# Finer background steps, weight splits shared with GpSimd, second buffers and earlier spatial operands in a hybrid gMLP and DeltaNet layer

## The chip, the cores and the metric

The program runs on one core of one Trainium2 chip. The metric is the device time of one execution, in microseconds (us); the kernel before took 2707.07 us, the median of three runs (2705.86, 2707.07, 2707.12). PE is TensorE, DVE is VectorE, ACT is ScalarE, POOL is GpSimd, and SP is the engine from whose queue the transfers are issued.

## The reference

One layer of a decoder works on 2048 new tokens of one sequence and on one new token of each of 8 other requests (the samples), with 1024 features. All products are in float32.

```python
h = rmsnorm(x, pre_g)
u_a, v_a, z_a, qkv, z_b, a_b, b_b, gate_a, gate_b = split(h @ w_in)
# branch A: inside chunks of 128 positions, 8 groups of 128 channels
vn = rmsnorm(v_a); y_a = u_a * (tril(w_s) @ vn + b_s) * silu(z_a)
# branch B: 8 heads of width 128
q, k, v = silu(causal_conv4(qkv)); q, k = l2norm(q) / sqrt(128), l2norm(k)
for t: S = a_t * S; S += k_t beta_t (v_t - S.T k_t).T; o_t = S.T q_t
y_b = rmsnorm(o) * silu(z_b)
out = x + rmsnorm((sigmoid(gate_a) * (y_a @ w_pa) + sigmoid(gate_b) * (y_b @ w_pb)) @ w_out)
```

The states, the last convolution rows and the samples' outputs are returned as well.

## The kernel before, in words

**The stream.** The bulk of PE's work is a stream of jobs. A job multiplies one 128-column block of a weight by the activations of half the tokens. Float32 is reached with three products in a rounded type: the weight is split into `hi` and `lo`, the activations into `Ah` and `Al`, and for each of 8 pieces of the 1024 features (k) `products` (L151) runs hi with Ah, hi with Al, and lo with Ah into one PSUM tile `acc` (L161). Half 0 has 1024 tokens, in two token blocks of 512 columns; half 1 has 1024 tokens and the 8 samples, in three blocks of 344. `split` (L141) makes `hi` on ACT (L147) and `lo` on DVE in two pieces of 128x512 (L149), for the next job, while the second token block of the present one runs. There are 185 splits.

**Background rounds.** Everything else is written as generators that yield between steps. `products` counts the columns that it has streamed, and each time the count passes `STRIDE` (2800) it calls `step`, which advances each of four queues once: `chq` (the chain), `smq` (statistics and samples), `cvq` (convolutions) and `bgq` (the rest, in order). Matrix products and transposes keep the program order on PE; a scheduler places the other engines' instructions, and from its own model it also sets how many `acc` products stand ahead of a background product.

**What runs in the background.** Per half: `v_mix` (L376), the spatial products of branch A. For each of 8 groups it fetches a triangular weight `wst` and a bias `bb` over the SP queue, masks `wst` on POOL (L407), scales a 128x1024 tile of v by its norm on POOL (L410), then runs four 128x128 products into `mx`, finishes them on DVE as `mo` (L418) and stores them. Then 8 heads, one after another (`head`, L424): transposes of k and q (`trn`), decays, key products `pk` (three products per chunk of 128 tokens, whose operands `kh` and `kl` are parted one chunk ahead on ACT L480 and POOL L481; `M` and `AT` come from `pk` on DVE, L494 and L495), scaling of q by the decays on POOL (L497), the inverse of a unit triangle (31 rounds of L511, L512, L513 on DVE, spread over 28 yields), and the merges (`g`, `p` and the POOL copies of `X`, L538 and L556). The merges start when `chq` is empty. The chain (L573) of a head then runs beside the next head: for each of 8 chunks three steps, `p` (product with the state S, then `r` on DVE, L585), `pz` (then `w` on ACT, L591) and `pu` (then the state S on DVE, L596), one step per round; after four chunks the output is normed, turned (`otr`) and finished as `yT` on DVE (L615), six rounds later.

```python
            yield
            pz = pg.tile([P, P], F32, tag="ch", name="pz", bufs=2)
            mm(pz, Y[:, c, :], r, start=True, stop=True)
            mm(O[:, n, :], qT[:, t], Sh, start=True, stop=False)
```

The convolutions of k, q and v run on DVE (L650, L653). In branch A the mixed rows are multiplied by silu(z) on POOL (L685). `samples` (L727) handles the 8 single tokens near the end. The opening (`v_phase`, L870, with L933 and L946) computes v of the first half while the first norms are still being made (`pr`, L245), and an end phase (from L1066, with L1100 and L1101) forms the outputs.

Of the kernel before, what the change touches and what calls it, by code (L numbers as in the profile page):

```python
# [15 lines left out]
P = 128  # L16
KB = 8
NH = 8
# [6 lines left out]
STRIDE = 2800  # L25
# [3 lines left out]
def hybrid_step(tc, d):  # L29
# [111 lines left out]
    def split(j):  # L141
        if j.hi is None:
            load(j)
            j.hi = wp.tile([P, KB, P], F32R, tag="hi", name="hi")
            j.lo = wp.tile([P, KB, P], F32R, tag="lo", name="lo")
            m = j.m
            nc.scalar.activation(j.hi[:, :, :m], j.raw[:, :, :m], AF.Copy)  # L147
            for p in (slice(0, 4), slice(4, 8)):
                nc.vector.tensor_tensor(j.lo[:, p, :m], j.raw[:, p, :m], j.hi[:, p, :m].bitcast(F32), ALU.subtract)  # L149
# [130 lines left out]
    # ======================= main phase =======================  # L280
# [4 lines left out]
    def btile(tag, dt=F32, shape=(P, 8, P)):  # L285
        return sp.tile(list(shape), dt, tag=tag, name=tag, bufs=2 if tag == "AT" else 1)
# [3 lines left out]
    # the 16 columns of a and b  # L290
# [85 lines left out]
    def v_mix(f, vts, ssv, sv):  # L376
        xv = sp.tile([P, 8], F32, tag="xv", name="xv")
        rv = sp.tile([P, 8], F32, tag="rv", name="rv")
        nc.vector.tensor_reduce(xv, ssv.rearrange("p (n g) -> p n g", n=8), AX.X, ALU.add)
        nc.vector.tensor_scalar(xv, xv, 1.0 / 1024, EPS, ALU.mult, ALU.add)  # L380
        rsqrt(rv, xv, 8)
        yield
        if f:
            sq = sp.tile([P, 64], F32, tag="sq", name="sq")
            nc.scalar.activation(sq, sv.rearrange("p g b -> p (g b)"), AF.Square)
            pc = pg.tile([P, 512], F32, tag="tr", name="pc")
            st = sp.tile([P, 16], F32, tag="st", name="st")[:, 0:NS]
            nc.vector.tensor_reduce(st, sq.rearrange("p (g b) -> p b g", b=NS), AX.X, ALU.add)
            yield
            mm(pc[:, 0:NS], ones, st, start=True, stop=True)  # L390
            xs = sp.tile([P, NS], F32, tag="xs", name="xs")
            rs = sp.tile([P, NS], F32, tag="rs", name="rs")
            nc.vector.tensor_scalar(xs, pc[:, 0:NS], 1.0 / 1024, EPS, ALU.mult, ALU.add)
            rsqrt(rs, xs, NS)
            nc.vector.tensor_tensor(sv, sv, rs.unsqueeze(1).to_broadcast([P, 8, NS]), ALU.mult)
            nc.vector.tensor_tensor(sv, sv, gmlpg.unsqueeze(2).to_broadcast([P, 8, NS]), ALU.mult)
            dma(d["o_vr"], sv)
            ms = sp.tile([P, 8, NS], F32, tag="ms", name="ms")
            nc.vector.tensor_tensor(ms, sv, ws00.unsqueeze(2).to_broadcast([P, 8, NS]), ALU.mult)
            nc.vector.tensor_tensor(ms, ms, bs0.unsqueeze(2).to_broadcast([P, 8, NS]), ALU.add)  # L400
            for g in range(8):
                dma(m_sp[f][g][:, HALF:HALF + NS], ms[:, g, :])
            yield
        for g in range(8):
            wst = sp.tile([P, P], F32, tag="r", name="wst", bufs=2)
            dma(wst, d["ws"][g])
            nc.gpsimd.affine_select(wst, wst, [[1, P]], ALU.is_ge, 0.0, base=0, channel_multiplier=-1)  # L407
            bb = sp.tile([P, P], F32, tag="w", name="bb", bufs=2)
            dma(bb, d["bs"][g:g + 1, :].partition_broadcast(P))
            nc.gpsimd.tensor_tensor(vts[g], vts[g], rv.unsqueeze(2).to_broadcast([P, 8, P]), ALU.mult)  # L410
            for _ in range(7 if g == 0 else 1):
                yield
            for gi in range(2):
                mx = pg.tile([P, 512], F32, tag="o" if gi == 0 else "kq", name="mx")
                for n in range(4):
                    mm(mx[:, n * P:(n + 1) * P], vts[g][:, gi * 4 + n, :], wst, start=True, stop=True)
                mo = sp.tile([P, 512], F32, tag="yT", name="mo", bufs=2)
                nc.vector.scalar_tensor_tensor(mo.rearrange("p (n t) -> p n t", t=P), mx.rearrange("p (n t) -> p n t", t=P), gmlpg[:, g:g + 1],  # L418
                                               bb.unsqueeze(1).to_broadcast([P, 4, P]), ALU.mult, ALU.add)
                dma(m_sp[f][g][:, gi * 512:(gi + 1) * 512], mo)  # L420
                yield

# [1 line left out]
    def head(f, h, T):  # L424
# [52 lines left out]
        def parted(c):  # L477
            kh = sp.tile([P, 2, P], F32R, tag="kh", name="kh", bufs=2)
            kl = sp.tile([P, 2, P], F32R, tag="kl", name="kl", bufs=2)
# [5 lines left out]
        yield  # L485
        for c in range(8):
            kh, kl = parts.pop()
            if c < 7:
                parted(c + 1)
# [10 lines left out]
        # inverse of the unit triangle: 32-blocks by substitution, then merged  # L500
# [8 lines left out]
        for l in range(31):  # L509
# [4 lines left out]
            if (l + 1) * 28 // 31 > l * 28 // 31:  # L514
                yield
# [3 lines left out]
        while chq:  # L519
            yield  # L520
        Y = btile("Y")
# [51 lines left out]
    def chain(f, h, kT, qT, KD, NV, AT, Y, T, bb, fe, eg, so):  # L573
        hcf = hc[f]
        col = lambda n, c: hcf[n][:, c * 8 + h:c * 8 + h + 1]
        Sh = S[:, h, :]
        for gi in range(2):
            O = pg.tile([P, 4, P], F32, tag="o", name="O")
            for n in range(4):
# [6 lines left out]
                yield  # L586
# [5 lines left out]
                yield  # L592
# [4 lines left out]
                yield  # L597
# [11 lines left out]
            for _ in range(6):  # L609
                yield  # L610
# [12 lines left out]
    def conv_job(f, kind, h, acts, T, after=None):  # L623
# [11 lines left out]
        def evac(b, ps, off, w):  # L635
# [5 lines left out]
            if f:  # L641
                nc.gpsimd.tensor_copy(qs[:, blk, :], raw[:, HALF + 3:HALF + 3 + NS])
            cvq.append(conv(raw))
# [18 lines left out]
    def zb_job(f, h, acts, T):  # L662
        def pre():
            T["zb"] = sp.tile([P, 1032], F32, tag="zb", name="zb", bufs=1)

        def evac(b, ps, off, w):
            zb = T["zb"]
            nc.scalar.activation(zb[:, off:off + w], ps[:, :w], AF.Silu)
            if b == 2 and f:
                nc.gpsimd.tensor_copy(zbs[:, h, :], zb[:, HALF:HALF + NS])  # L670

# [55 lines left out]
    def samples():  # L727
        while "E" not in ended:
# [45 lines left out]
        # pairs (k, q) per head and sample  # L774
# [40 lines left out]
        yield  # L815
        nc.vector.tensor_tensor(sq[:, 0:64], o, o, ALU.mult)
# [52 lines left out]
    # v of the first half comes with tokens on the partitions, straight from the products  # L869
    def v_phase(A, vt_tile, st):  # L870
        spans = [(0, 1), (1, 2), (2, 4), (4, 6), (6, 8)]
        tags = [("Y", 1), ("NV", 1), ("KD", 2), ("KD", 2), ("craw", 2), ("craw", 2), ("AT", 2), ("vT", 1)]
# [15 lines left out]
        def stage(cv, i):  # L888
            if i == 0:
                t = flat(wp.tile([P, KB, P], F32, tag="raw", name="raw", bufs=1))  # L890
            elif cv == 0 and i == 1:
                t = sp.tile([P, 1032], F32, tag="zb", name="wraw")
# [95 lines left out]
    def half(f):  # L988
# [7 lines left out]
        def vt_tile(g):  # L996
# [4 lines left out]
            return sp.tile([P, 1032], F32, tag="zb", name="vt7", bufs=1)[:, 0:HALF].rearrange("p (n c) -> p n c", c=P)  # L1001
# [63 lines left out]
    # ======================= end phase =======================  # L1065
# [179 lines left out]
```

## Time and profile before

| what | value |
|---|---|
| runs | 2705.86, 2707.07, 2707.12 us |
| profiled execution, span | 2705.5 us |
| PE busy | 2615.8 us (97%), 15755 matmuls |
| DVE busy | 1553.0 us (57%) |
| ACT busy | 1044.4 us (39%) |
| POOL busy | 420.7 us (16%) |
| mean granted TensorE clock | 0.987 of full speed |

The profiled execution took 2705.5 us from its first instruction to its last; the median of the runs is 1.6 us above that span. Busy times are sums over the instructions of an engine; the clock is what the throttle granted TensorE, as a share of full speed.

### The profile page before, as it was taken

How to read it: one execution, taken by the hardware profiler on the slowest of the kernel's cores; microseconds unless marked ns; L12 is line 12 of the kernel's file. 1: busy time of each engine (PE TensorE's matmuls, PEld its weight loads, DVE VectorE, ACT ScalarE, POOL GpSimd, SP SyncE). 2: the span in 40 equal slices, each digit the busy share in tenths (PEclk: the TensorE clock that was granted, in tenths of full speed). 3: DMA queues.
4: the chain of work that ended last, by engine and by line, in shares of the span. 5: the costliest groups of instructions: out<-in, count | busy, mean ns of one | idle time of the engine just before them, and what ended most of it. 6: DMA issues, size and time to landing. Idle time of an engine off the chain costs nothing.

```text
span 2705.5 us, 42484 instructions
## 1 busy us (share of the span) xinstructions
PE 2615.8 (97%) x15755; PEld 2334.3 (86%) x15755; DVE 1553.0 (57%) x5001; ACT 1044.4 (39%) x2728; POOL 420.7 (16%) x535
## 2 busy tenths in 40 slices
PE   7989999999999999989999999999998999999998
PEld 6778788887788888989999999999998988999886
DVE  6266866765765725356668657567565444442454
ACT  5323453453453423423534534534431332332121
POOL 2021111121121102022112211211202102102000
PEclk9989999999999999999999999999999999999999
DMA  6232212211211223123122122112145676645442
GB/s 205 79 121 63 67 43 71 86 44 59 79 44 67 86 77 115 48 70 108 56 65 68 48 76 72 42 68 75 46 133 202 221 245 233 243 168 183 136 141 95
DMA packets 139792, 280.38 MB, mean 104 GB/s; under 512 B 19944, under 2 KB 75688, under 8 KB 139584
## 3 DMA queue, kind: packets, MB, share of 16 engines
q1 hardware_dynamic: 139584, 277.66, 31.0%
q8 instruction: 124, 2.03, 0.3%
q14 instruction: 84, 0.69, 0.1%
HBM read 205.06 MB, written 72.55 MB: 103 GB/s over the span
## 4 chain that ended last, share of the span: by engine, by line
PE 78%; DVE 11%; DMA 5%; ACT 3%; issue 1%; POOL 1%; SPq 0%; DVEq 0%; ACTq 0%; POOLq 0%
PE acc L161 64%; PE p L32 2%; PE acc L933 2%; PE O L32 2%; DVE vT L653 2%; PE trn L33 2%; PE pu L32 1%; PE g L32 1%; DVE lo L149 1%; PE pz L32 1%; PE pk L32 1%; DMA m<-mo 1%; DVE bc L511 1%; DVE nwt L96 1%; DMA xt<-in_x_tok 1%
## 5 line engine op out<-in xcount | busy, mean ns | idle before, releaser
L161 PE MATMUL acc<-Ah,hi 128*128 128x344 f32 (+1 forms) x3360 | 1202.2, 358 | 1.4 <-ACT Ah L203 1.4
L161 PE MATMUL acc<-Ah,lo 128*128 128x344 f32 (+1 forms) x3360 | 1201.0, 357 | 0.3 <-DVE lo L149 0.3
L161 PE MATMUL acc<-Al,hi 128*128 128x344 f32 (+1 forms) x3360 | 1199.4, 357 | 0.5 <-DVE Al L204 0.2
L161 PEld LDWEIGHTS acc<-Al,hi 128*128 128x128 f32 x3360 | 636.1, 189 | 57.7 <-DVE Al L204 1.4
L161 PEld LDWEIGHTS acc<-Ah,lo 128*128 128x128 f32 x3360 | 636.6, 189 | 57.1 <-DVE lo L149 0.6
L161 PEld LDWEIGHTS acc<-Ah,hi 128*128 128x128 f32 x3360 | 636.2, 189 | 57.1 <-ACT Ah L203 1.9
L149 DVE TENSOR_TENSOR lo<-raw,hi 128x512 fp32r<-128x512 f32 x370 | 266.3, 739 | 313.4 <-ACT hi L147 278.8
L147 ACT ACTIVATE hi<-raw 128x1024 fp32r<-128x1024 f32 x185 | 195.3, 1056 | 320.6 <-PE acc L161 282.8
L513 DVE TENSOR_TENSOR Yc<-Yc,tmp 128x248 f32<-128x248 f32 (+30 forms) x496 | 148.6, 300 | 10.2
L511 DVE STREAM_SHUFFLE bc<-Uc 128x248 f32<-128x248 f32 (+30 forms) x496 | 151.1, 309 | 0.0
L512 DVE TENSOR_TENSOR tmp<-bc,Yc 128x248 f32<-128x248 f32 (+30 forms) x496 | 145.7, 294 | 0.5
L481 POOL TENSOR_TENSOR kl<-kq,kh 128x256 fp32r<-128x256 f32 x128 | 97.9, 773 | 238.1 <-ACT kh L480 237.9
L653 DVE SCALAR_TENSOR_TENSOR kq<-craw,convw,kq 128x1024 f32<-128x1024 f32 x96 | 122.6, 1277 | 1.1
L591 ACT ACTIVATE w<-pz,s_bb 128x128 f32<-128x128 f32 x128 | 46.9, 367 | 184.4 <-PE pz L32 184.1
L585 DVE SCALAR_TENSOR_TENSOR r<-p,neg,NV 128x128 f32<-128x128 f32 x128 | 44.2, 346 | 126.7 <-PE p L32 126.2
L161 PE MATMUL acc<-Bh,hi 128*128 128x344 f32 (+1 forms) x320 | 111.9, 350 | 0.0
L161 PE MATMUL acc<-Bh,lo 128*128 128x344 f32 (+1 forms) x320 | 111.9, 350 | 0.0
L161 PE MATMUL acc<-Bl,hi 128*128 128x344 f32 (+1 forms) x320 | 111.6, 349 | 0.0
L1101 POOL TENSOR_TENSOR g<-g,u 128x344 f32<-128x344 f32 (+1 forms) x40 | 45.1, 1128 | 349.1 <-DVE g L1100 344.9
L637 ACT ACTIVATE craw<-acc 128x344 f32<-128x344 f32 (+1 forms) x120 | 61.1, 509 | 94.1 <-PE acc L161 93.8
L446 ACT ACTIVATE junk<-trn 128x128 f32<-128x128 f32 x256 | 67.4, 283 | 42.3 <-PE trn L33 42.3
L1100 DVE TENSOR_TENSOR g<-g,acc 128x344 f32<-128x344 f32 (+1 forms) x40 | 23.2, 581 | 101.6 <-PE acc L161 83.5
(321 smaller groups left out, 3485.3 us busy)
## 6 DMA issues: line engine op xcount, KB each, us to landing
raw<-in_w_blk SPq DMA_DIRECT2D x136, 512.0 KB, 3.7
g<-big SPq DMA_DIRECT2D x16, 516.0 KB, 3.2
g<-g SPq DMA_DIRECT2D x16, 516.0 KB, 4.8
xt<-in_x_tok SPq DMA_DIRECT2D x16, 512.0 KB, 4.8
m<-mo SPq DMA_DIRECT2D x32, 256.0 KB, 3.1
G<-gc SPq DMA_DIRECT2D x16, 512.0 KB, 9.0
g<-big SPq DMA_DIRECT2D x16, 512.0 KB, 2.8
yb<-yT SPq DMA_DIRECT2D x32, 256.0 KB, 2.3
```

The source lines that it names most:

```text
L32: mm = lambda *a, **k: tc.keep_in_program_order(nc.tensor.matmul(*a, **k))
L33: transpose = lambda *a, **k: tc.keep_in_program_order(nc.tensor.transpose(*a, **k))
L147: nc.scalar.activation(j.hi[:, :, :m], j.raw[:, :, :m], AF.Copy)
L149: nc.vector.tensor_tensor(j.lo[:, p, :m], j.raw[:, p, :m], j.hi[:, p, :m].bitcast(F32), ALU.subtract)
L161: nc.tensor.matmul(out, wt[:, k, :j.m], at[:, k, off:off + w], start=(i == 0), stop=(i == 23))
L446: nc.scalar.activation(junk, tr[:, tk(n)], AF.Square, accum_out=acc[:, c:c + 1])
L481: nc.gpsimd.tensor_tensor(kl, kq[:, :, tk(c)], kh.bitcast(F32), ALU.subtract)
L511: nc.vector.stream_shuffle(bc[:, :, l + 1:], Uc[:, :, l + 1:], [l] * 32)
L512: nc.vector.tensor_tensor(tmp[:, :, l + 1:], bc[:, :, l + 1:], Yc[:, :, l:l + 1].to_broadcast([P, 8, 31 - l]), ALU.mult)
L513: nc.vector.tensor_tensor(Yc[:, :, l + 1:], Yc[:, :, l + 1:], tmp[:, :, l + 1:], ALU.subtract)
L637: nc.scalar.activation(raw[:, 3 + off:3 + off + w], ps[:, :w], AF.Copy)
L653: nc.vector.scalar_tensor_tensor(acc, raw[:, i:i + HALF], convw[:, blk, i:i + 1], acc, ALU.mult, ALU.add)
```

## The change

- `STRIDE` falls from 2800 to 2000 columns, so background rounds come more often. The chain yields `LAG` = 2 times where it yielded once, and waits 8 rounds where it waited 6.
- In `split` the second piece of `lo` (k 4 to 7) is made by GpSimd and no longer by DVE.
- `Y`, `NV` and `zb` have two buffers, `kh` and `kl` three, and the key operands are parted two chunks ahead.
- The inverse yields after each of its 31 rounds. The merges of a head start when one chain or none is left in `chq`, and no longer when none is.
- `v_mix` fetches the operands of group g+1 before the products of group g, and yields evenly, twice per group.
- `samples` waits on flags for what it reads, since its order against the rest is looser. The last lines free some SBUF for the buffers.

```diff
-STRIDE = 2800
+STRIDE = 2000
+LAG = 2
...
-            for p in (slice(0, 4), slice(4, 8)):
-                nc.vector.tensor_tensor(j.lo[:, p, :m], j.raw[:, p, :m], j.hi[:, p, :m].bitcast(F32), ALU.subtract)
+            for eng, p in ((nc.vector, slice(0, 4)), (nc.gpsimd, slice(4, 8))):
+                eng.tensor_tensor(j.lo[:, p, :m], j.raw[:, p, :m], j.hi[:, p, :m].bitcast(F32), ALU.subtract)
...
-        return sp.tile(list(shape), dt, tag=tag, name=tag, bufs=2 if tag == "AT" else 1)
+        return sp.tile(list(shape), dt, tag=tag, name=tag, bufs=2 if tag in ("AT", "Y", "NV") else 1)
...
-        for g in range(8):
+        def fetch(g):
             wst = sp.tile([P, P], F32, tag="r", name="wst", bufs=2)
...
-            for _ in range(7 if g == 0 else 1):
+            return wst, bb
+
+        yield
+        got = fetch(0)
+        for _ in range(8):
+            yield
+        for g in range(8):
+            wst, bb = got
+            if g < 7:
+                got = fetch(g + 1)
+            for gi in range(2):
                 yield
-            for gi in range(2):
...
-            kh = sp.tile([P, 2, P], F32R, tag="kh", name="kh", bufs=2)
-            kl = sp.tile([P, 2, P], F32R, tag="kl", name="kl", bufs=2)
+            kh = sp.tile([P, 2, P], F32R, tag="kh", name="kh", bufs=3)
+            kl = sp.tile([P, 2, P], F32R, tag="kl", name="kl", bufs=3)
...
         parted(0)
         yield
+        parted(1)
+        yield
         for c in range(8):
-            kh, kl = parts.pop()
-            if c < 7:
-                parted(c + 1)
+            kh, kl = parts.pop(0)
+            if c < 6:
+                parted(c + 2)
...
-            if (l + 1) * 28 // 31 > l * 28 // 31:
+            if True:
                 yield
...
-        while chq:
-            yield
+        while len(chq) > 1:
+            yield
+        yield
...
+        def lag():
+            for _ in range(LAG):
+                yield
+
...
-                yield
+                yield from lag()
                 pz = pg.tile([P, P], F32, tag="ch", name="pz", bufs=2)
...
-            for _ in range(6):
+            for _ in range(8):
                 yield
             tr = pg.tile([P, 512], F32, tag="tr", name="otr")
...
-            T["zb"] = sp.tile([P, 1032], F32, tag="zb", name="zb", bufs=1)
+            T["zb"] = sp.tile([P, 1032], F32, tag="zb", name="zb", bufs=2)
...
-        while "E" not in ended:
+        while "E" not in ended or any(("qs", b) not in ended for b in range(24)):
             yield
...
-    nc = bacc.Bacc("TRN2", target_bir_lowering=False, num_devices=1)
+    nc = bacc.Bacc("TRN2", target_bir_lowering=False, num_devices=1, dynamic_dma_scratch_size=1024)
```

The instruction streams show three things that the diff does not. In the changed kernel line numbers are higher: L149, L161, L410 and L933 of before are L150, L162, L411 and L955. First, PE in a chain of half 0: `p` is the product with the state, `pz` the next step, whose operand `r` DVE makes in between; `acc` are the stream's products. Before:

```order
L32 MATMUL p_2835<-S,kq 128x128
L161 MATMUL acc<-Al,hi 128x512
L161 MATMUL acc<-Ah,lo 128x512
L161 MATMUL acc<-Ah,hi 128x512
L161 MATMUL acc<-Al,hi 128x512
L161 MATMUL acc<-Ah,lo 128x512
L32 MATMUL pz<-r,Y 128x128
```

And with the change:

```order
L33 MATMUL p_3222<-S,kq 128x128
L162 MATMUL acc<-Ah,hi 128x512
L162 MATMUL acc<-Al,hi 128x512
L162 MATMUL acc<-Ah,lo 128x512
L162 MATMUL acc<-Ah,hi 128x512
L162 MATMUL acc<-Al,hi 128x512
L162 MATMUL acc<-Ah,lo 128x512
L162 MATMUL acc<-Ah,hi 128x512
L162 MATMUL acc<-Al,hi 128x512
L33 MATMUL pz<-r,Y 128x128
```

Eight products of the stream stand between two chain steps where five stood (five or six in most places before, eight now). Second, POOL around the scaling of v in half 0, before:

```order
L204 TENSOR_TENSOR Al<-big,Ah 128x256 x4
L410 TENSOR_TENSOR E<-E,rv 128x1024
L410 TENSOR_TENSOR G<-G,rv 128x1024
L410 TENSOR_TENSOR M<-M,rv 128x1024
L410 TENSOR_TENSOR AT<-AT,rv 128x1024
L410 TENSOR_TENSOR Y<-Y,rv 128x1024
L410 TENSOR_TENSOR NV<-NV,rv 128x1024
L410 TENSOR_TENSOR vt_721<-vt_721,rv 128x1024
L410 TENSOR_TENSOR vt_722<-vt_722,rv 128x1024
L640 COPY hist<-craw 128x3
```

And with the change:

```order
L205 TENSOR_TENSOR Al<-big,Ah 128x256 x4
L535 MEMSET Y 128x1024
L150 TENSOR_TENSOR lo<-raw,hi 128x512 x2
L411 TENSOR_TENSOR E<-E,rv 128x1024
L411 TENSOR_TENSOR G<-G,rv 128x1024
L411 TENSOR_TENSOR M<-M,rv 128x1024
L411 TENSOR_TENSOR AT<-AT,rv 128x1024
L411 TENSOR_TENSOR Y<-Y,rv 128x1024
L411 TENSOR_TENSOR NV<-NV,rv 128x1024
L411 TENSOR_TENSOR vt_721<-vt_721,rv 128x1024
L411 TENSOR_TENSOR vt_722<-vt_722,rv 128x1024
L150 TENSOR_TENSOR lo<-raw,hi 128x512
```

The eight scalings still stand in one row on POOL, and pieces of `lo` have come in ahead of them and behind them. Third, PE in the opening: `pr` spreads the norms of the last tokens over the partitions, and `acc` with `wvhi`, `wvlo`, `wvh` and `wvl` are the first half's v. The last `pr` of the opening, before:

```order
L933 MATMUL acc_525<-wvhi_172,Ah_168 128x512
L933 MATMUL acc_525<-wvhi_172,Al_169 128x512
L933 MATMUL acc_525<-wvlo_174,Ah_168 128x512
L32 MATMUL pr_546<-cst_72,rx_81 128x128 x2
L933 MATMUL acc_525<-wvhi_172,Ah_168 128x512
```

And with the change:

```order
L955 MATMUL acc_506<-wvh_175,Ah_168 128x512
L955 MATMUL acc_506<-wvh_175,Al_169 128x512
L955 MATMUL acc_506<-wvl_176,Ah_168 128x512
L33 MATMUL pr_510<-cst_72,rx_81 128x128 x2
L955 MATMUL acc_571<-wvhi_171,Ah_168 128x512
```

The last `pr` has moved to the end of a row of v products; it stood nine products later, inside the next row.

## Rows read from the trace of the kernel before

**Rows 1.** PE's waits: engine, line, what it waited for, total us, times, longest.
```profile
PE p L32 <- DVE S L596: 14.9, 9, 4.6
PE pz L32 <- DVE r L585: 13.8, 10, 2.9
PE mx L32 <- DVE mo L418: 11.2, 3, 6.6
...
PE mx L32 <- DVE rx L98: 8.3, 1, 8.3
...
PE pk L32 <- DVE yT L615: 3.9, 4, 1.2
PE g L32 <- POOL X L556: 2.9, 4, 1.2
PE otr L33 <- ACT OS L608: 2.5, 2, 1.5
PE pk L32 <- DVE nwt L97: 1.8, 1, 1.8
PE pk L32 <- POOL kl L481: 1.5, 2, 1.1
```
**Rows 2.** Windows of 50 us: busy us (instructions) of each engine, clock, DMA share, GB/s.
```profile
2550.00:2600.00 50.00, 50.00 (x217) 40.38 (x216) 24.61 (x76) 10.91 (x23) 0.00 (x0) 1.00 0.42 138
```
**Rows 3.** The same view, two windows with chains in which the clock fell.
```profile
300.00:350.00 50.00, 46.66 (x220) 38.22 (x220) 40.65 (x171) 15.31 (x38) 6.97 (x9) 0.97 0.24 64
...
2050.00:2100.00 50.00, 43.95 (x281) 42.81 (x280) 29.68 (x93) 10.44 (x28) 7.50 (x4) 0.93 0.70 243
```
**Rows 4.** Timeline 307 to 312.4 us: start us, us, engine, line, operation, out<-in, [idle before].
```profile
307.00 0.42 DVE L513 TENSOR_TENSOR Yc<-Yc,tmp 128x248 f32<-128x248 f32 x1
...
307.68 1.52 POOL L685 TENSOR_TENSOR big<-big,t 128x512 f32<-128x512 f32 x1 [5.57 <-ACT t L683]
...
308.09 1.38 DVE L513 TENSOR_TENSOR Yc<-Yc,tmp 128x240 f32<-128x240 f32 x1
...
310.01 0.68 DVE L149 TENSOR_TENSOR lo<-raw,hi 128x512 fp32r<-128x512 f32 x1
...
311.88 0.34 DVE L585 SCALAR_TENSOR_TENSOR r<-p,neg,NV 128x128 f32<-128x128 f32 x1
...
312.27 0.38 PE L32 MATMUL pz<-r,Y 128*128 128x128 f32 x1 [2.10 <-DVE r L585]
```
**Rows 5.** The page's costliest groups: the `lo` pieces on DVE.
```profile
L149 DVE TENSOR_TENSOR lo<-raw,hi 128x512 fp32r<-128x512 f32 x370 | 266.3, 739 | 313.4 <-ACT hi L147 278.8
```
**Rows 6.** Groups of POOL by form: xcount | busy us, mean ns | idle before.
```profile
L685 POOL TENSOR_TENSOR big<-big,t 128x512 f32<-128x512 f32 x16 | 21.7, 1356 | 97.7 <-ACT t L683 97.7
```
**Rows 7.** Timelines at the spatial products, halves 0 and 1.
```profile
129.08 1.90 POOL L410 TENSOR_TENSOR E<-E,rv 128x1024 f32<-128x1024 f32 x1 [75.94 <-DVE rv L98]
...
142.17 1.82 DVE L98 SCALAR_TENSOR_TENSOR rx<-nwt,rx 128x9 f32<-128x9 f32 x1
...
147.11 1.19 PE L32 MATMUL mx<-wst,G 128*128 128x128 f32 x4 [8.25 <-DVE rx L98]
...
1213.81 0.75 DVE L418 SCALAR_TENSOR_TENSOR mo<-mx,vecs,bb 128x512 f32<-128x512 f32 x1 [4.65 <-DMA m<-mo]
```
**Rows 8.** Timeline of the opening.
```profile
45.68 0.28 DVE L946 COPY M<-acc 128x128 f32<-128x128 f32 x1
...
46.18 0.68 PE L32 MATMUL pr<-cst,rx 128*128 128x128 f32 x4
```
**Rows 9.** Timeline 493 to 545 us: last key product, inverse's end, first merge.
```profile
493.23 0.28 PE L32 MATMUL pk<-kh,kl 128*128 128x256 f32 x1
...
528.34 0.45 DVE L517 STREAM_TRANSPOSE Xc<-Yc 128x256 f32<-128x256 f32 x1
...
543.44 1.09 PE L32 MATMUL g<-Xc,M 32*32 32x32 f32 x32
```

More of the change, by code (lines that the diff above doesn't have):

```diff
@@ L591, in chain @@
                 nc.scalar.activation(w, pz, AF.Copy, scale=bb[:, c:c + 1])
-                yield
+                yield from lag()
                 pu = pg.tile([P, P], F32, tag="ch", name="pu", bufs=2)
@@ L596, in chain @@
                 nc.vector.scalar_tensor_tensor(Sh, Sh, eg[:, c:c + 1], pu, ALU.mult, ALU.add)
-                yield
+                yield from lag()
             OS = sp.tile([P, 4, P], F32, tag="OS", name="OS")
@@ L642, in evac @@
                 nc.gpsimd.tensor_copy(qs[:, blk, :], raw[:, HALF + 3:HALF + 3 + NS])
+                ended.add(("qs", blk))
             cvq.append(conv(raw))
@@ L670, in evac @@
                 nc.gpsimd.tensor_copy(zbs[:, h, :], zb[:, HALF:HALF + NS])
+                ended.add(("zbs", h))
         return Job(wblk(48 + h), acts, TBS[f], evac, pre)
@@ L815, in samples @@
         yield
+        while any(("zbs", h) not in ended for h in range(NH)):
+            yield
         nc.vector.tensor_tensor(sq[:, 0:64], o, o, ALU.mult)
@@ L871, in v_phase @@
         spans = [(0, 1), (1, 2), (2, 4), (4, 6), (6, 8)]
-        tags = [("Y", 1), ("NV", 1), ("KD", 2), ("KD", 2), ("craw", 2), ("craw", 2), ("AT", 2), ("vT", 1)]
+        tags = [("Y", 2), ("NV", 2), ("KD", 2), ("KD", 2), ("craw", 2), ("craw", 2), ("AT", 2), ("vT", 1)]
         def x_tile(i):
@@ L891, in stage @@
             elif cv == 0 and i == 1:
-                t = sp.tile([P, 1032], F32, tag="zb", name="wraw")
+                t = sp.tile([P, 1032], F32, tag="zb", name="wraw", bufs=2)
             else:
@@ L1000, in vt_tile @@
                 return sp.tile([P, 8, P], F32, tag="KD", name="vt6", bufs=2)
-            return sp.tile([P, 1032], F32, tag="zb", name="vt7", bufs=1)[:, 0:HALF].rearrange("p (n c) -> p n c", c=P)
+            return sp.tile([P, 1032], F32, tag="zb", name="vt7", bufs=2)[:, 0:HALF].rearrange("p (n c) -> p n c", c=P)
         groups = []
```

## The prediction

> **What bounds the kernel now.** I read the engines' busy time first: PE is busy for 2615.8 of 2705.5 us, so at most some 90 us can be had without taking products away, and the change takes none away. I then read where PE idles [rows 1]. Three kinds matter. The chain's two waits, `p` for the state and `pz` for `r`, make 14.9 + 13.8 = 28.7 us in 19 stalls. Five smaller kinds around the key products, the merges and the output transposes make 3.9 + 2.9 + 2.5 + 1.8 + 1.5 = 12.6 us. The spatial products wait 11.2 + 8.3 = 19.5 us. Most of the rest is the opening.
>
> Next, what a full-speed stretch looks like: 217 matmuls in 50 us at clock 1.00 [rows 2], so one 512-column product takes 0.231 us. After a stall the clock is lower for a while. Seven 50 us windows with chains and without spatial products show it: six at 0.97, the first of which is shown, and one at 0.93 [rows 3]. They lose about 6 x 1.5 + 3.5 = 12.5 us beside the waits themselves. [...]
>
> Last, why the chain waits at all, since `r` itself takes 0.34 us. The timeline of one stall [rows 4] shows it. L513 takes 0.42 us at 307.00, but 1.38 us at 308.09, when a POOL product over two SBUF tiles (L685, from 307.68, 1.52 us) runs: L513 ends as that ends. So a POOL operation holds a DVE operation with two SBUF inputs, here for 0.96 us, and `r`, queued behind L513, `lo` and others, starts only at 311.88; PE has idled for 2.10 us by then. **The kernel is bound by PE, with small losses where DVE's queue is late for a chain step that stands only five or six products away.**
>
> **The change part by part.**
>
> *Chain spacing.* In the new order eight products stand between chain steps, where five or six stood. That gives two to three products of 0.231 us [rows 2], on average 0.58 us, to each of the 19 stalls [rows 1]: 19 x 0.58 = **-11.0 us**. The bounds are 0, if DVE is later by as much, and all 28.7 us.
>
> *Half of `lo` on POOL.* Each of 185 splits takes one piece of 0.74 us [rows 5] off DVE, and puts one on POOL. The trace has no `lo` on POOL; the nearest row is L685, the same 128x512 with two SBUF inputs, mean 1.36 us [rows 6]. So DVE does 185 x 0.74 = 137 us less and POOL 185 x 1.36 = 252 us more, both off PE's path. What counts is what stands ahead of `r`: 0.74 us less work, against a hold of up to 1.36 us when the POOL piece runs just then. I take these as cancelling: **0**. For one stall the bounds are -0.74 and +0.62 us, over 19 stalls -14 and +12 us. [...]
>
> *Key operands two ahead, second buffers, merges.* PE's waits for `kl` (1.5) and for `X` (2.9) [rows 1] should go: `kl` is made a chunk earlier, and in the new order the merges no longer lie beside the k convolution on DVE. **-4.4 us**, bounds 0 and -12.6. The waits for `yT`, `OS` and `nwt` (8.2 us) are DVE and ACT being late for other reasons; they stay. The second buffers for Y, NV and zb take no wait of PE's list away by themselves; they let the merges of one head overlap the chain of the one before, and cost nothing on PE.
>
> *The inverse.* Its rounds now come faster: counted in the order, 8.3 us fewer products stand between the last key product and the first merge. In the trace these were 543.44 - 493.23 = 50.2 us apart, and DVE finished its part at 528.34 + 0.45, 35.6 us after the key product [rows 9]. So 41.9 us stay for a DVE stretch of 35.6 us: slack of 6.3 us, enough for four POOL holds of 1.36 us even if nothing is saved. **0**, and a loss only beyond that.
>
> *Clock.* I scale the 12.5 us by the share of waits that go, 15.4 of 28.7 + 12.6 = 41.3: **-4.7 us**.
>
> *Spatial products.* The 8.25 us stall at 138.9 comes from eight POOL scalings in a row, 1.90 us each from 129.08; the rsqrt on DVE is held 1.82 us per small operation, and `mo` stands behind it [rows 7]. In the new order the eight scalings still stand in a row and the rsqrt still stands ahead of `mo` on DVE. So fetching ahead does not reach this, nor its twin of 6.6 us in half 1 [rows 1]. The two other stalls (11.2 - 6.6 = 4.6 us) come from `mo` waiting for its previous store (4.65 us at 1213.81 [rows 7]). Fetching ahead moves two SP transfers and one POOL mask per group in front of that store; it removes none. **0**; the bounds are -8 us (4.6 and about 3.4 of clock) and +3, if each of the stores is late by as much again as half that wait.
>
> *Opening.* The last `pr` needs a norm that is ready at 45.68 + 0.28 plus a little, and it starts at 46.18 without a wait [rows 8]. It now stands nine products earlier, so PE must wait about 9 x 0.231 = **+2.1 us**; bounds 0 and +3.
>
> *Extra interruptions* of the stream (finer rounds) cost nothing, since the number of products on PE is the same.
>
> **Sum.** -11.0 - 4.4 - 4.7 + 2.1 = -18.0 us. Span 2705.5 - 18.0 = 2687.5; the runs lie 1.6 us above the span, so **2689 us**.
>
> **The rivals.**
>
> *All chain waits go.* Spacing and a lighter DVE queue could cover each hold. Then 41.3 us of waits, 12.5 of clock and 8 at the spatial products go: 2705.5 - 61.8 + 2.1 = 2645.8, **2647 us** as a run. For it: without the one of 4.6 us the 19 stalls average 1.34 us ((28.7 - 4.6) / 18), and DVE's queue gets 0.74 us lighter at each split. Against: a stall of 2.10 us [rows 4] and one of 4.6 us [rows 1] are far longer than 0.58 us of spacing. Chance 0.17.
>
> [...] POOL gets 252 us of work that can hold DVE, where it had 421 us in all. Per head there are 136 block jobs / 16 = 8.5 splits. If 2.5 of them hold DVE by 0.96 us [rows 4] just ahead of a chain step, PE loses 2.5 x 16 x 0.96 = 38 us, and by the ratio 12.5 / 41.3 another 12 us of clock: 2687.5 + 50 = 2737.5, **2739 us**. It decides from about 0.9 such stalls per head (18.0 / (16 x 0.96 x 1.3)). For it: the hold that was seen [rows 4]. Against: it needs POOL to start before DVE's own piece, and the steps now have 1.85 us (8 x 0.231) of cover where they had 1.2 to 1.4. Chance 0.22.
>
> *Nothing much changes.* The holds take back just what the spacing gives, and only `kl` and `X` go: -4.4 - 1.3 of clock + 2.1 = -3.6; span 2701.9, **2703.5 us**. That the change does not do what it says belongs here: for the spatial fetch it seems so already, for the chain the order shows the wider spacing. Chance 0.20.
>
> **How the numbers follow.** My forecast has a chance of 0.41. A measurement of this kernel can tell about 0.2% from no change, 5.4 us: 2701.7 to 2712.5 is "same". Faster: 0.40 of the forecast, all 0.17 of the first rival, 0.07 of the last: 0.64. Same: 0.01 of the forecast, 0.02 of the second, 0.13 of the last: 0.16. Slower: 0.20 of the second. The range must leave out no more than 0.2. Down to 2652 it takes in the forecast with its bounds and much of the first rival; up to 2725 it takes in the last rival and the milder half of the slower one. The forecast's own range is 2671 to 2705: -14 and +12 us of the `lo` term, times 1.3 for the clock.
>
> **What would show it.** Right: PE's wait list has `p` and `pz` together near 18 us (28.7 before), `kl` and `X` near nothing, `mx` near 19, `pr` up by 2; DVE's busy time falls by some 130 us and POOL's grows by some 250. Wrong: `p` and `pz` above 28.7, with DVE operations of two SBUF inputs stretched beside a POOL `lo` in the stalls (the second rival), or a new wait of `acc` for the POOL piece of `lo`, or `g` waiting for `Xc` because the shorter inverse is not done.

## The result, and the profile after

The changed kernel took 2780.39 us (median of four runs, 2776.74 to 2786.08), against 2707.1 us before: a ratio of 1.0276, 95% interval 1.0260 to 1.0291 (the two medians alone give 1.0271). It is slower by 73 us by the medians and 75 by the ratio, where I had forecast 18 us less, and it lies above my range of 2652 to 2725 us.

The page of the changed kernel begins so (busy us, share of the span, instructions):

```profile
PE 2653.3 (95%) x15755; PEld 2347.8 (84%) x15755; DVE 1506.0 (54%) x4816; ACT 1052.7 (38%) x2732; POOL 686.4 (25%) x720
```

The span is 2780.7 us, so PE idles for 127.4 us where it idled for 89.7: +37.7. PE's busy time has grown too, from 2615.8 to 2653.3: +37.5, for the same 15755 matmuls. The cores' row tells most of that second half:

```profile
core 0: 2780.7 us, clock 0.979
```

The clock was 0.987 before. By my estimate from these two rows, (1 - 0.979) x 2780.7 = 58.4 us are lost to it, against 35.2: +23.2 us. Some 14 us of longer PE busy time stay unexplained.

The waits of PE, after, answer to [rows 1]:

```profile
PE mx L33 <- DVE mo L428: 23.8, 4, 10.2
PE trn L34 <- ACT NV L544: 14.4, 8, 4.1
PE p L33 <- DVE S L614: 13.3, 19, 1.1
PE pr L33 <- DVE rx L99: 11.7, 3, 8.2
PE pz L33 <- DVE r L603: 11.2, 19, 2.6
PE trn L34 <- ACT junk L456: 8.2, 8, 1.5
PE trn L34 <- ACT kq L674: 7.2, 11, 1.0
PE otr L34 <- ACT OS L626: 6.1, 7, 2.1
```

The wait of `g` for `X` is gone, and `p` and `pz` fell a little, from 28.7 to 24.5 us, but in 38 stalls in place of 19. The transposes `trn`, which waited for 0.8 us before, now wait for 29.8 us on ACT (14.4 + 8.2 + 7.2), and on ACT only as the last link. Their two rows before:

```profile
PE trn L33 <- ACT NV L531: 0.6, 1, 0.6
...
PE trn L33 <- DVE KD L456: 0.2, 1, 0.2
```

Two places show what stands behind.

The timeline of the changed kernel around 243 us and 249 to 256 us (start us, us, engine, line, operation, [idle before]), in the first head:

```profile
243.75 1.29 POOL L150 TENSOR_TENSOR lo<-raw,hi 128x512 fp32r<-128x512 f32 x1 [9.89 <-ACT hi L148]
243.83 1.28 DVE L524 TENSOR_TENSOR tmp<-bc,Yc 128x48 f32<-128x48 f32 x1
...
249.13 3.92 DVE L672 SCALAR_TENSOR_TENSOR kq<-craw,convw,kq 128x1024 f32<-128x1024 f32 x3
...
253.08 1.06 ACT L674 ACTIVATE kq<-kq 128x1024 f32<-128x1024 f32 x1 [3.15 <-DVE kq L672]
254.04 1.13 ACT L544 ACTIVATE NV<-trn,s_nk 128x128 f32<-128x128 f32 x4
...
255.22 1.11 PE L34 MATMUL trn<-cst,vT 128*128 128x128 f32 x4 [3.66 <-ACT NV L544]
```

The GpSimd piece of `lo` runs from 243.75 to 245.04, and the inverse's L524, whose neighbours take 0.20 to 0.21 us, ends 0.07 us after it: a hold of 1.07 us. The inverse, the last thing ahead of the convolution on DVE, ends later by that; the convolution of the next head runs until 253.05, ACT's SiLU (L674) waits for it, and `NV`, which needs nothing from it, stands behind the SiLU on ACT. So the second transpose of v waits for 3.66 us. The hold is only a part of that: with `lo` on DVE (run `lo_on_dve` below) DVE runs the convolution ahead of the last rounds of the inverse, and the same transpose waits for 0.72 us. From the last part of the wait on, the clock was halved (windows view; busy us by engine, clock, DMA share, GB/s):

```profile
254.40:267.80 13.40, 12.58 (x86) 9.39 (x86) 2.12 (x3) 5.07 (x13) 2.38 (x3) 0.50 0.00 1
```

That is 13.4 us at 0.50: by estimate half of it, 6.7 us, on top of a wait of 3.66.

The second place, in a middle head, same columns:

```profile
489.69 2.18 POOL L491 TENSOR_TENSOR kl<-kq,kh 128x256 fp32r<-128x256 f32 x3 [1.23 <-ACT kh L490]
...
490.49 0.70 DVE L97 TENSOR_TENSOR nwt<-rko 128x4 f32<-128x4 f32 x1
491.22 0.67 DVE L98 SCALAR_TENSOR_TENSOR nwt<-nwt,s_so 128x4 f32<-128x4 f32 x1
...
492.12 1.14 ACT L626 ACTIVATE OS<-O,rko 128x128 f32<-128x128 f32 x4 [1.64 <-DVE rko L99]
...
494.09 0.66 PE L34 MATMUL trn<-cst,kq 128*128 128x128 f32 x4 [1.55 <-ACT junk L456]
```

Here `kl`, which was on GpSimd before the change too, stretches small DVE operations of the output norm from 0.14 to 0.70 us; ACT's `OS` waits for them, and the squares `junk`, which would free the transposes' PSUM tile, stand behind `OS`. Five of the eight waits of `trn` for `junk` are of this kind, 1.54 to 1.55 us each, one per head in the later heads of half 0; the other three, in half 1, are under 0.2 us each.

### The profile page after: what moved, and what is told of

The parts are those of the page before. It is cut to its first block, busy times and chain, and to the rows that moved or that the text cites. A ratio compares the mean times of both kernels' runs of the same rounds, so it can differ in the third digit from the quotient of the medians.

```text
span 2780.7 us, 42702 instructions
## 1 busy us (share of the span) xinstructions
PE 2653.3 (95%) x15755; PEld 2347.8 (84%) x15755; DVE 1506.0 (54%) x4816; ACT 1052.7 (38%) x2732; POOL 686.4 (25%) x720
## 4 chain that ended last, share of the span: by engine, by line
PE 63%; DVE 22%; ACT 5%; DMA 4%; issue 2%; POOL 1%; SPq 0%; DVEq 0%; ACTq 0%; POOLq 0%
PE acc L162 51%; DVE bc L523 3%; DVE Yc L525 3%; DVE tmp L524 3%; DVE kq L672 2%; PE p L33 2%; DVE lo L150 2%; DVE vT L672 2%; PE pk L33 2%; PE O L33 1%; PE g L33 1%; PE acc L955 1%; ACT hi L148 1%; PE pu L33 1%; DMA xt<-in_x_tok 1%
## 5 line engine op out<-in xcount | busy, mean ns | idle before, releaser
L162 PE MATMUL acc<-Ah,hi 128*128 128x344 f32 (+1 forms) x3360 | 1206.6, 359 | 3.5 <-ACT Ah L204 3.0
L162 PE MATMUL acc<-Ah,lo 128*128 128x344 f32 (+1 forms) x3360 | 1207.1, 359 | 0.0
L162 PE MATMUL acc<-Al,hi 128*128 128x344 f32 (+1 forms) x3360 | 1205.0, 359 | 2.0 <-POOL Al L205 1.5
L162 PEld LDWEIGHTS acc<-Ah,hi 128*128 128x128 f32 x3360 | 639.3, 190 | 60.3 <-ACT Ah L204 3.8
L162 PEld LDWEIGHTS acc<-Al,hi 128*128 128x128 f32 x3360 | 639.4, 190 | 59.2 <-POOL Al L205 1.8
L162 PEld LDWEIGHTS acc<-Ah,lo 128*128 128x128 f32 x3360 | 639.8, 190 | 56.8
L150 POOL TENSOR_TENSOR lo<-raw,hi 128x512 fp32r<-128x512 f32 x185 | 292.6, 1582 | 1207.4 <-ACT hi L148 1130.1
L150 DVE TENSOR_TENSOR lo<-raw,hi 128x512 fp32r<-128x512 f32 x185 | 155.9, 843 | 299.3 <-ACT hi L148 280.8
L525 DVE TENSOR_TENSOR Yc<-Yc,tmp 128x248 f32<-128x248 f32 (+30 forms) x496 | 168.4, 340 | 9.6
L524 DVE TENSOR_TENSOR tmp<-bc,Yc 128x248 f32<-128x248 f32 (+30 forms) x496 | 153.8, 310 | 0.5
L162 PE MATMUL acc<-Bh,hi 128*128 128x344 f32 (+1 forms) x320 | 111.9, 350 | 0.0
L162 PE MATMUL acc<-Bh,lo 128*128 128x344 f32 (+1 forms) x320 | 111.9, 350 | 0.0
L162 PE MATMUL acc<-Bl,hi 128*128 128x344 f32 (+1 forms) x320 | 111.6, 349 | 0.0
L614 DVE SCALAR_TENSOR_TENSOR S<-S,s_eg,pu 128x128 f32<-128x128 f32 x128 | 43.6, 340 | 106.5 <-PE pu L33 106.3
```

Source lines behind the costliest of these rows:

```text
L150: eng.tensor_tensor(j.lo[:, p, :m], j.raw[:, p, :m], j.hi[:, p, :m].bitcast(F32), ALU.subtract)
L162: nc.tensor.matmul(out, wt[:, k, :j.m], at[:, k, off:off + w], start=(i == 0), stop=(i == 23))
L524: nc.vector.tensor_tensor(tmp[:, :, l + 1:], bc[:, :, l + 1:], Yc[:, :, l:l + 1].to_broadcast([P, 8, 31 - l]), ALU.mult)
L525: nc.vector.tensor_tensor(Yc[:, :, l + 1:], Yc[:, :, l + 1:], tmp[:, :, l + 1:], ALU.subtract)
```

## The experiments

I had two theories. **P**: the GpSimd piece holds DVE, as it held L524 for 1.07 us above, and DVE's lateness reaches PE. The expectations call this theory the shared port, or the port; the runs show the lengthening, and not that a port is shared. **R**: the finer rounds make a yield worth 2000 columns in place of 2800, so background products stand closer to what they need. All ratios are to the kernel before on the same chip; 1% is 27 us. Waits and busy times are from the one profiled execution of each run.

### Both parts undone, singly and together

Run `lo_on_dve`, the changed kernel with:

```diff
-            for eng, p in ((nc.vector, slice(0, 4)), (nc.gpsimd, slice(4, 8))):
+            for eng, p in ((nc.vector, slice(0, 4)), (nc.vector, slice(4, 8))):
```

> The changed kernel with both pieces of lo back on DVE; all else as changed. If the shared port is the cause (theory P: each GpSimd piece holds DVE operations with two SBUF inputs), most of the 73 us goes: 2700 to 2715 us, the transposes' waits (trn, 30 us in the changed kernel) fall under 8 us, and L525 falls from 340 back to about 300 ns. If the finer rounds are the cause (theory R: background products stand fewer stream products behind what they need, whoever makes lo), little goes: 2760 to 2785 us, and trn still waits over 20 us.

Run `old_rounds`, the changed kernel with:

```diff
-STRIDE = 2000
-LAG = 2
+STRIDE = 2800
+LAG = 1
...
-            for _ in range(8):
+            for _ in range(6):
```

> The changed kernel with the old rounds (STRIDE 2800, one chain yield per step, six rounds before otr); lo half on GpSimd, buffers, key operands two ahead, early fetch stay. Theory R: trn waits under 5 us, the clock's loss back to that of before, 2705 to 2725 us. Theory P: the holds stay, trn and chain still wait, 2745 to 2785 us.

Run `rest_alone`, both edits together:

> Neither the GpSimd piece nor the finer rounds: the buffers, the key operands two ahead, the inverse's 31 yields, merges beside a chain, the early fetch and the moved pr. Both theories: 2700 to 2715 us, within about 0.3% of before. If it is clearly slower (over 2725), a third part of the change is to blame, the fetch or the merges beside a chain.

Run `lo_split_alone`, the kernel before with GpSimd making the second piece of `lo`:

> The kernel before with the second piece of lo on GpSimd, nothing else. Theory P: 2740 to 2775 us, with waits of p, pz, pk, g well over the 41 us of before. Theory R: 2700 to 2715 us. My prediction's term for this part was 0, with bounds of -14 and +12 us.

| kernel | lo, second piece | columns per round | ratio, 95% interval |
|---|---|---|---|
| changed | GpSimd | 2000 | 1.0276 (1.0260 to 1.0291) |
| `lo_on_dve` | DVE | 2000 | 1.0026 (1.0014 to 1.0038) |
| `old_rounds` | GpSimd | 2800 | 1.0058 (1.0035 to 1.0082) |
| `rest_alone` | DVE | 2800 | 0.9899 (0.9878 to 0.9920) |
| `lo_split_alone`, all else as before | GpSimd | 2800 | 1.0117 (1.0093 to 1.0142) |

Both theories hold a part, and neither all of it. In units of 27 us per 1%: the rest gains 27 us; finer rounds alone add 34 (0.0127); the GpSimd piece alone adds 43 (0.0159), and 32 in the kernel before; both together add 102, that is 25 us more than their sum. So -27 + 34 + 43 + 25 makes the 75 us of the result, and with finer rounds already there the GpSimd piece costs 43 + 25 = 68 us. I had given the three parts -4, -11 and 0 us, clock and opening apart. The expectation for `rest_alone` (no change) was a miss on the good side, and for `lo_split_alone` both ranges missed (2736 us lies just under P's and far above R's). P was right on the time of `lo_on_dve` (2711 us) and on L525 (340 ns in the changed kernel, 297 there), and wrong on its transposes; R was right on the time of `old_rounds` (2719 us), where P had told 2745 or more. R's low waits of `trn` came true in `old_rounds` (1.1 + 0.7 us), and P's chain waits as well: 15.0 + 5.8 us for `pz` and `p`, against 7.6 + 0.4 in `rest_alone`. In `lo_on_dve` the transposes still waited, which is R's own part:

```profile
PE mx L33 <- DVE mo L428: 13.5, 3, 6.5
...
PE trn L34 <- ACT NV L544: 8.4, 9, 1.6
PE trn L34 <- ACT junk L456: 6.1, 6, 1.2
PE mx L33 <- DVE nwt L97: 5.7, 1, 5.7
PE pz L33 <- DVE r L603: 5.0, 9, 1.3
PE p L33 <- DVE S L614: 4.2, 5, 1.8
```

`p` and `pz` make 9.2 us here where they made 28.7 before. It is tempting to call that the work of the wider spacing, but `rest_alone`, whose chain steps stand five or six products apart as before, has less still:

```profile
PE pz L33 <- DVE r L603: 7.6, 6, 2.7
...
PE p L33 <- DVE S L614: 0.4, 1, 0.4
```

So the rest took these waits down, and neither pair shows a gain from the wider spacing: 8.0 to 9.2 us with `lo` on DVE, 20.8 to 24.5 with the GpSimd piece. `STRIDE` and `LAG` were not changed apart, so what the spacing alone is worth stays open.

DVE's busy time is the other reading of this run:

```profile
PE 2622.2 (97%) x15755; PEld 2330.2 (86%) x15755; DVE 1497.4 (55%) x5001; ACT 1057.6 (39%) x2736; POOL 396.9 (15%) x535
```

With both pieces of `lo` DVE is busy for 1497.4 us, and in the changed kernel, with 185 pieces fewer, for 1506.0.

### What holds DVE: GpSimd's reads

Run `extra_reads`, the kernel before with work that nobody needs on GpSimd (its result goes to a scratch tile):

```diff
+            if m == P:
+                ex = wp.tile([P, 4, P], F32, tag="ex", name="ex", bufs=1)
+                nc.gpsimd.tensor_tensor(ex, j.raw[:, 4:8, :], j.hi[:, 4:8, :].bitcast(F32), ALU.subtract)
```

> The kernel before, both pieces of lo on DVE, plus one useless subtraction of 128x512 per split on GpSimd (reads raw and hi, writes a scratch tile that nobody reads). Theory P (the shared port): 2725 to 2765 us, DVE operations with two SBUF inputs longer on average. If the loss came only from who makes lo and when (order, PE waiting for the piece), nothing waits for this piece and the time stays within 0.3% of before.

Run `extra_writes`, the kernel before with a GpSimd write of about the same length in its place:

```diff
+            if m == P:
+                nc.scalar.activation(ext, j.hi[:, 0, 0:1].bitcast(F32), AF.Copy, scale=ex[:, 0:1])
+                nc.gpsimd.memset(ex, 0.0)
```

Both runs also have the smaller DMA scratch of the changed kernel, to make room; in the second, `ex` is cleared once more at the start.

> The kernel before plus one memset of 128x1408 per split on GpSimd, tied to hi by a one-column ACT instruction: about the same 1.3 us of GpSimd per split, but no read of SBUF. Theory P (a hold needs GpSimd to read SBUF): within 0.5% of before, and clearly under the run with extra reads. If GpSimd's own queue being late (kl, X) is what costs, it is as slow as the run with extra reads.

Ratios: 1.0185 (1.0159 to 1.0210) with the reads, 1.0028 (1.0018 to 1.0039) with the writes: 50 us against 8, both as P told. The first row of the page of each, reads first:

```profile
PE 2638.0 (96%) x15755; PEld 2342.5 (85%) x15755; DVE 1705.9 (62%) x5001; ACT 1042.4 (38%) x2728; POOL 727.9 (26%) x719
```

and writes:

```profile
PE 2609.7 (96%) x15755; PEld 2326.4 (86%) x15755; DVE 1568.6 (58%) x5001; ACT 1082.2 (40%) x2912; POOL 649.0 (24%) x720
```

DVE runs the same 5001 instructions as before, and its busy time is 1705.9 us with the reads, against 1553.0 before: 153 us of being held, 0.83 us per split. With the writes it is 1568.6. GpSimd's own busy time rises by 307 us with the reads and by 228 with the writes (420.7 before), so its queue is filled in both, if not equally, and the 153 us of DVE show in the reads alone: it is the read, not the queue. By groups, mean ns of one instruction before, with the reads and with the writes: `lo`, which reads two tiles of SBUF, takes 742, 975 and 740; the inverse's `tmp` at 128x192, two tiles as well, 376, 507 and 377; its `bc` at 128x240, which reads one, 450, 450 and 451; `M` and `AT`, which read `pk` in PSUM, 345, 345 and 346, and 279, 278 and 279. In these groups the reads lengthen what has two SBUF inputs, but that is not all: the first product of the convolution, `kq`, which reads one tile and a column, takes 779, 1139 and 1000. It is longer with the writes too, and the runs do not tell why. PE's list of `extra_reads` has no wait for `lo`, and of those for `hi` only the 0.8 us of before, so late weights are not the cause either.

### What the finer rounds cost

Run `late_turns`, the run with `lo` on DVE and, in the head:

```diff
-        for _ in range(0):
+        for _ in range(4):
             yield
...
+            yield
             squares(turned(qT, "kq", gi), gi, ssq)
...
-        yield
+        for _ in range(4):
+            yield
         Y = btile("Y")
```

with one more yield after the squares of q also.

> The run with lo on DVE and the finer rounds, with more yields in the head: four more before the first transposes, one more after each of them, three more before the merges, so that about as many stream columns stand there as with 2800 per round. Theory R, told more exactly (a yield that was worth 2800 columns is worth 2000, so conv, SiLU and squares are not done when the transposes come): trn waits fall from 14.5 us to under 4 and the time from 2711 to 2690 to 2700 us. If the rounds cost through something else (more interruptions of the stream, the spatial products), it stays at 2705 or more.

Measured 0.9986 (0.9976 to 0.9996), 2703 us, between what R told and the other range: `trn` fell from 14.5 to 3.1 us as expected, but only 11 us came back, since `pz` rose from 5.0 to 15.9 us and `pu` to 4.3. The spatial products stayed as slow (`mx` 13.8 + 7.1 us). So the turns are a part of R, not all.

Run `late_turns_spread`, the same with this edit, which lets the scaling of group g wait for the products of group g-2, so that the eight no longer stand in a row:

```diff
-            nc.gpsimd.tensor_tensor(vts[g], vts[g], rv.unsqueeze(2).to_broadcast([P, 8, P]), ALU.mult)
+            nc.gpsimd.tensor_tensor(vts[g % 2], vts[g], rv.unsqueeze(2).to_broadcast([P, 8, P]), ALU.mult)
...
-                    mm(mx[:, n * P:(n + 1) * P], vts[g][:, gi * 4 + n, :], wst, start=True, stop=True)
+                    mm(mx[:, n * P:(n + 1) * P], vts[g % 2][:, gi * 4 + n, :], wst, start=True, stop=True)
```

> Finer rounds with lo on DVE and the later transposes (ratio 0.9986), and the scalings of v spread. It tells what of the finer rounds' cost lies at the spatial products: if the 20.9 us of mx waits there go and the clock with them, 0.988 to 0.991, still over the 0.987 of the old rounds with spread scalings, the difference being chain and merge waits. If finer rounds cost through the interruptions of the stream themselves, 0.994 or more.

Measured 0.9884 (0.9867 to 0.9901), as expected if the cost lies at the spatial products. And run `spread_scaling`, the same edit on `rest_alone`:

> The rest alone (ratio 0.990 to before) with the eight scalings of v on GpSimd spread: the scaled tile of group g goes into the tile of group g-2, so it has to wait for that group's products, and the eight no longer stand in a row. If the row of eight holds the rsqrt on DVE by the port and mo behind it (my reading of the trace before), PE's mx waits fall from 9.3 us to under 4 and the ratio to 0.985 to 0.988. If the spatial products wait for stores or weights instead, the waits stay near 9 and the ratio near 0.990.

Measured 0.9871 (0.9858 to 0.9884). PE has no wait of `mx` left in its list here, and 1.6 + 0.9 us in `late_turns_spread`. Finer rounds thus cost 34 us as they stand (0.9899 to 1.0026), and 4 us, inside the intervals, once the turns are later and the scalings spread (0.9871 to 0.9884). The larger part was at the spatial products: the edit gives 28 us with finer rounds, and 8 with the old ones, so some 20 of the 30 us that were had back.

### The early fetch

Run `rest_old_fetch`: `rest_alone` with the old lines of `v_mix` put back (fetch, mask and scaling of group g inside its own turn, one yield, no yield between the two products).

> The rest alone (2676.5 us) with the old spatial part, no fetch ahead. If the early fetch gave the rest's gain at the spatial products (their waits were 19.5 us before, 9.3 in the rest alone, and the clock was lower for less long), 2688 to 2700 us. If the two second buffers and the merges beside a chain gave it, 2674 to 2684 us. My prediction gave the fetch 0.

Measured 0.9945 (0.9925 to 0.9966), against 0.9899: the fetch and the even yields give 12 us, a bit under half of the rest's gain, and 2690 us is in the range told for it. PE's `mx` waits are 8.9 + 8.1 + 2.1 us with the old lines and 9.3 in `rest_alone`. The other 15 us are less clear. At the chain `p` and `pz` wait for 14.3 us with the old lines and for 8.0 in `rest_alone`, where they waited for 28.7 before; but the key products wait more than before, and PE idles only 7.6 us less in all (82.1 against 89.7). PE's busy time is 12.1 us shorter, with the clock at 0.993 in place of 0.987. Which of the buffers or yields does that was not tried.

### A miss, and a version that beats both

Run `late_norm`: `spread_scaling` with the ten operations of the k norm moved behind the key products.

> The run with the spread scalings, and the ten small operations of the k norm's rsqrt moved from ahead of the key products to behind them. In the rest alone PE's key products wait 9.3 + 2.5 us for these operations (pk for nwt), because M and AT stand behind them on DVE. If that is so, these waits fall under 4 us and the ratio falls by another 0.003; if the operations then delay the inverse and the merges, g or trn shows a new wait and the ratio stays.

Measured 0.9965 (0.9953 to 0.9977), worse by 25 us. The key products' wait stayed at 9.2 us, so those operations were not the k norm's; moved to the inverse they delayed the chain (`pz` 24.7 us in place of 8.1), where I had looked for a new wait of `g` or `trn`. The timeline of `spread_scaling` told which they were, the output norm of the running chain, and what stretched them (GpSimd's rows first, then DVE's):

```profile
408.53 0.76 POOL L491 TENSOR_TENSOR kl<-kq,kh 128x256 fp32r<-128x256 f32 x1
409.37 2.36 POOL L509 TENSOR_TENSOR kq<-kq,G 128x1024 f32<-128x1024 f32 x1
...
409.69 2.06 DVE L97 TENSOR_TENSOR nwt<-rko 128x4 f32<-128x4 f32 x1
411.68 0.28 DVE L507 TENSOR_TENSOR AT<-pk,E 128x128 f32<-128x128 f32 x1
411.88 0.15 DVE L98 SCALAR_TENSOR_TENSOR nwt<-nwt,s_so 128x4 f32<-128x4 f32 x1
```

An operation on 4 columns takes 2.06 us beside GpSimd's L509, and 0.15 us without it. It ends with L509, and `AT` (L507) stands behind it; the next key product waits for that, for 2.07 us. Run `keys_on_dve` takes these two reads off GpSimd:

```diff
-            nc.gpsimd.tensor_tensor(kl, kq[:, :, tk(c)], kh.bitcast(F32), ALU.subtract)
+            nc.vector.tensor_tensor(kl, kq[:, :, tk(c)], kh.bitcast(F32), ALU.subtract)
...
-        nc.gpsimd.tensor_tensor(qT, qT, flat(G), ALU.mult)
+        nc.vector.tensor_tensor(qT, qT, flat(G), ALU.mult)
```

> The run with the spread scalings (ratio 0.987), and the low part of the key operands and the scaling of q by the decays made on DVE, no longer on GpSimd. In the run with the spread scalings PE's key products wait about 19 us for DVE, whose small operations of the output norm last up to 2.06 us in place of 0.15 beside GpSimd's reads there. If the port is what stretches them, these waits fall under 8 us and the ratio to 0.980 to 0.984. If DVE's own load is what counts, its 50 to 70 us more work there costs at least as much and the ratio is 0.987 or more.

Measured 2647.45 us, ratio 0.9777 (0.9762 to 0.9791): 60 us faster than before, and more than the 0.980 to 0.984 that I expected. The page:

```profile
PE 2599.0 (98%) x15755; PEld 2325.2 (88%) x15755; DVE 1530.2 (58%) x5145; ACT 1051.0 (40%) x2728; POOL 279.7 (11%) x391
```

DVE has 144 instructions more than in `spread_scaling`, and its busy time is 1530.2 us against 1539.5: it does more work and still ends up less busy, because it is held less. The small operations L97 of the output norm show it: they last 0.33 us on average in `spread_scaling` and 0.18 here. What is left of PE's waits at the chain and the keys:

```profile
PE p L33 <- DVE S L614: 4.6, 2, 2.6
...
PE pz L33 <- DVE r L603: 3.7, 5, 1.3
PE pk L33 <- DVE AT L507: 2.4, 1, 2.4
```

In `spread_scaling` the key products waited 19.0 us for DVE:

```profile
PE pk L33 <- DVE nwt L98: 9.3, 7, 2.1
...
PE pk L33 <- DVE rko L99: 3.8, 4, 1.5
...
PE pk L33 <- DVE AT L507: 3.4, 3, 1.6
...
PE pk L33 <- DVE nwt L97: 2.5, 2, 1.2
```

They fell to 2.4.

## Why the prediction was wrong, by its own steps

Two steps made the loss, the first one below and the finer rounds further down. Either of them alone turns the 27 us that the rest gains into a small loss (1.0058 and 1.0026). A third, the chain spacing, is not borne out.

- *Half of `lo` on POOL: 0, bounds -14 and +12.* **This step failed.** I set 0.74 us less DVE work against a hold of up to 1.36 us and let them cancel, over the 19 stalls that existed. Measured alone it costs 32 us in the kernel before, 43 us in the changed one with old rounds, and 68 us on top of the finer rounds. Three things were missed. A piece takes 1.58 us on GpSimd on average, not 1.36 (row below): at 467.07 us one lasts 1.80 us where DVE's own piece began 0.04 us earlier, against the 1.29 us of the timeline above, so the hold runs both ways: DVE's piece took 0.69 us there, and 1.82 at 190.16, where GpSimd's had begun 0.01 us earlier and took 1.28. The piece makes new stalls: 37 of `p` and `pz` in `lo_split_alone` where there were 19, 40.5 us in place of 28.7. And that growth of 11.8 us, just my bound, is only about half of the 21.5 us by which PE idles longer in that run; `trn` (4.9 us in place of 0.8) and `mx` (23.0 in place of 19.5) wait longer too, and the term had nothing for them.

```profile
L150 POOL TENSOR_TENSOR lo<-raw,hi 128x512 fp32r<-128x512 f32 x185 | 292.6, 1582 | 1207.4 <-ACT hi L148 1130.1
L150 DVE TENSOR_TENSOR lo<-raw,hi 128x512 fp32r<-128x512 f32 x185 | 155.9, 843 | 299.3 <-ACT hi L148 280.8
```

DVE's own piece lasts 0.84 us in place of 0.74 [rows 5], so 185 pieces fewer took only 110 us off it (266.3 to 155.9), and DVE's busy time fell by 47 us, from 1553.0 to 1506.0, not by 130. Against `lo_on_dve`, which differs in this part alone, it even rose by 8.6 us: there the holds cost DVE more than the work that was taken away. With the old rounds it fell, but only by 25.5 us (`rest_alone` to `old_rounds`) and 13.3 (before to `lo_split_alone`).

- *Chain spacing: -11.0.* Not borne out. The chain waits fall from 28.7 to 8.0 us in `rest_alone` without any wider spacing, and do not fall further with it (9.2 in `lo_on_dve`). Where the GpSimd piece is added they come back, to 20.8 with the old rounds and 24.5 with the finer ones. The fall that I forecast was there, but from other parts of the change.
- *Extra interruptions (finer rounds): nothing.* **The second step that failed: 34 us.** I counted the distance from the last key product to the first merge, where indeed nothing waits for `Xc`, and left the others unpriced: from the convolution to the transposes of k and q, and from the inverse to those of v. That is 29.8 us of waits in the changed kernel, 14.5 of it with `lo` on DVE. I called the finer interruptions free; within the intervals they were (the 4 us between `spread_scaling` and `late_turns_spread`), but the shorter distances, at the transposes and at the spatial products, were not.
- *Spatial products: 0, bounds -8 and +3.* Wrong in both directions. With old rounds the early fetch gave 12 us. With finer rounds the spatial products stand closer together, and the row of eight scalings, which I rightly saw unmoved, cost more: `mx` waits for 9.3 us in `rest_alone`, 19.4 with finer rounds (`lo_on_dve`) and 25.7 in the changed kernel, 19.5 before.
- *Key operands and merges: -4.4.* `X` went as told (2.9 us); `kl` stayed (1.4 us) in the changed kernel, and both are gone in `rest_alone`.
- *Clock: -4.7.* With the waits up the sign turned, and the ratio was too small as well: by 12.5 / 41.3 the 37.7 us of longer idling would have cost 11.4 us, and the loss grew by 23.2. The 12.5 us were only a part of the 35.2 us lost before, and a window was missed: 2000 to 2050 us, which has chain steps too, also stands at 0.97.
- *Opening: +2.1.* Right: `pr` waits for 11.7 us, and for 9.6 before and in `rest_alone`, where the last `pr` stands where it stood before.
- The second rival had the hold and the side, with a chance of 0.22, and 2739 us was too little. It priced only stalls of the chain, where the holds also reached the transposes by way of ACT, whose instructions stood in line behind one that waited for DVE.

The signs that I named would not have told: `p` and `pz` stayed under 28.7 us, and no `acc` waits for the POOL piece and no `g` for `Xc`. The waits had moved to `trn`, which the prediction does not mention, and more stood at `mx`.

What stays open: what the wider spacing alone gives, which part of the rest took the chain waits down, how the 25 us that the two parts cost together beyond their sum divide among the stalls, and the 14 us of PE busy time that the clock does not explain. By the same working `lo_on_dve` has some 15 us of it too (2622.2 us at 0.990) and `late_turns` 1 us (2619.5 at 0.986), so it came with the finer rounds and went with the later turns, whoever made `lo`.

## What to carry to other kernels

Moving work to GpSimd was not paid in GpSimd time here: price it by the DVE operations that run beside it and lengthen (in `extra_reads` `lo`, with two SBUF inputs, went from 742 to 975 ns), and by what stands in line behind them, and check by DVE's busy time, which should fall by the work that was taken away (here 137 us of pieces, and it fell by 47). A spacing that is counted in yields changes every distance in the program when a yield gets shorter, so list all distances, not the one that it was made for. Where a burst of GpSimd reads can be spread by a dependence that is there anyway, or moved to DVE outright, DVE can end up less busy than with the help (1530.2 us in `keys_on_dve`, 1539.5 in `spread_scaling`).

## What was not expected of the hardware

- A DVE operation on 4 columns per partition lasted 2.06 us beside a GpSimd product over 1024, against 0.15 us for its neighbour without one; beside `kl` pieces of 0.73 us it was 0.70. In these places the length of the other's instruction counted, not its own.
- 184 useless GpSimd subtractions added 153 us to DVE's busy time, more than the 136 us that DVE would have needed for the same pieces at 0.74 us each.
- A wait of PE of 3.66 us was followed by 13.4 us at half clock, by estimate a loss of 6.7 us, where the lower clock cost 0.03 of a 50 us window before, or 1.5 us [rows 3].
